# Seven pairs of transposes moved from TensorE to VectorE, and a head that runs zero matmuls and loads tile by tile, in a matmul with subtraction

## The chip, the cores and the metric

The kernel runs on one core of a Trainium2 chip. The metric is device microseconds of one execution, as the median of several runs. The profiled execution is one more run, and its span goes from its first to its last instruction.

## The reference

```python
def setup_inputs():
    batch, m, k, n = 16, 512, 1024, 768
    # x (16, 512, 1024), weight (1024, 768), sub_value (16, 512, 768), all float32
def reference(x, weight, sub_value):
    return (np.matmul(x, weight) - sub_value).astype(np.float32)
```

With batch and m flattened, this is an 8192 x 1024 by 1024 x 768 product, from which an 8192 x 768 array is subtracted. In bytes: 33.6 MB of x, 3.1 MB of weight and 25.2 MB of sub_value are read, and 25.2 MB of output are written.

## The kernel before

The 8192 rows are cut into 64 tiles of 128 rows ("m tiles", numbered by `mi`), and four neighbouring m tiles make a group (16 groups). TensorE contracts over partitions, so each tile of x has to be turned: ScalarE casts it from f32 to f16 (`cast`, L97), the engine that is to turn it sees pairs of f16 as one f32 word (so a tile is 128 x 512 words, four 128 x 128 blocks), TensorE transposes the four blocks against an identity matrix into PSUM (`transposes`, L105), and ScalarE copies the turned tile back to SBUF (L112). Even and odd k are then separate stripes of the turned tile. The weight is loaded so that it matches: each of its four chunks has even and odd rows side by side, and VectorE casts it to f16 (L76).

A tile's product is four chunks (`matmuls(mi, c)`), each of four matmuls of 128 x 384 (two stripes by two halves of n), summed in one of three PSUM buffers. `finish` (L144, VectorE) subtracts sub_value in place in its own SBUF tile `so_tile`, which is then stored.

The order on every engine is the order of the code (`keep` holds it). The head works on tiles 0, 1 and 2 together, chunk by chunk as the weights arrive. The main loop runs over `mi` from 3: at each first tile of a group SP issues the load of x three groups ahead (`XA`), of sub_value two groups ahead (`SA`), and a store `OA` groups behind; then come the four chunks of tile `mi`, with one transposed block of tile `mi + 2` (`TA`) behind each chunk; then the cast of tile `mi + 4` (`TA + CA`) and `finish(mi)`. All transfers are on SP's one queue. They take turns on eight completion semaphores, and the ninth is issued only when the first has landed. The x pool holds four groups, so a group's load also waits until ScalarE has cast the whole group four before it. `transposes_dve` exists but has no tile in `ON_DVE`.

Of the kernel before, what the change touches and what calls it, by code (L numbers as in the profile page):

```python
# [8 lines left out]
P = 128  # L9
Q = 32  # L10
F32 = mybir.dt.float32
F16 = mybir.dt.float16

S = 8
G = 4
XA, SA, OA = 3, 2, 1
TA = 2
CA = 2
HEAD = 3
ON_DVE = frozenset()  # L20


@with_exitstack
def kernel(
    ctx: ExitStack,
    tc: tile.TileContext,
    x: bass.AP,
    weight: bass.AP,
    sub_value: bass.AP,
    out: bass.AP,  # L30
):
    nc = tc.nc
    keep = tc.keep_in_program_order

    x_flat = x.flatten_outer_dims()
    sub_flat = sub_value.flatten_outer_dims()
    out_flat = out.flatten_outer_dims()

    M_TOT, K = x_flat.shape
    _, N = weight.shape  # L40
    n_mt = M_TOT // P
    n_g = n_mt // G
    NS = N // 2
    KW = K // 2
    n_c = KW // P

    x_s = x_flat.rearrange("(s p j) k -> s p j k", p=P, j=S)
    sub_s = sub_flat.rearrange("(s p j) n -> s p j n", p=P, j=S)
    out_s = out_flat.rearrange("(s p j) n -> s p j n", p=P, j=S)
    w_c = weight.rearrange("(c p r) n -> c p r n", p=P, r=2)  # L50

    def rows(view, mi, n):
        return view[mi // S][:, mi % S : mi % S + n]

    const_pool = ctx.enter_context(tc.tile_pool(name="const", bufs=1))
    w_pool = ctx.enter_context(tc.tile_pool(name="w_pool", bufs=1))
    x_pool = ctx.enter_context(tc.tile_pool(name="x_pool", bufs=4))
    x16_pool = ctx.enter_context(tc.tile_pool(name="x16_pool", bufs=CA + 2))
    xt_pool = ctx.enter_context(tc.tile_pool(name="xt_pool", bufs=TA + 3))
    so_pool = ctx.enter_context(tc.tile_pool(name="so_pool", bufs=6))  # L60
    psum_t_pool = ctx.enter_context(tc.tile_pool(name="psum_t", bufs=2, space=bass.MemoryType.PSUM))
    psum_o_pool = ctx.enter_context(tc.tile_pool(name="psum_o", bufs=3, space=bass.MemoryType.PSUM))

    ident = const_pool.tile([P, P], F32)
    make_identity(nc, ident)


    w_sb = w_pool.tile([P, n_c, 2, N], F16)

    x_t, so_t, x16_t, xt_t, ps_t, po_t = {}, {}, {}, {}, {}, {}  # L70

    def load_w(c):
        st = so_pool.tile([P, 2, N], F32, name="w_stage", tag="so_tile")
        keep(nc.sync.dma_start(out=st, in_=w_c[c]))
        for r in range(2):
            keep(nc.vector.tensor_copy(out=w_sb[:, c, r], in_=st[:, r]))  # L76

    def load_x(mi, n):
        g, j = divmod(mi, G)
        if j == 0:  # L80
            x_t[g] = x_pool.tile([P, G, K], F32, name="x_tile")
        keep(nc.sync.dma_start(out=x_t[g][:, j : j + n], in_=rows(x_s, mi, n)))

    def load_sub(mi, n):
        g, j = divmod(mi, G)
        if j == 0:
            so_t[g] = so_pool.tile([P, G, N], F32, name="so_tile")
        keep(nc.sync.dma_start(out=so_t[g][:, j : j + n], in_=rows(sub_s, mi, n)))

    def store(mi, n):  # L90
        g, j = divmod(mi, G)
        keep(nc.sync.dma_start(out=rows(out_s, mi, n), in_=so_t[g][:, j : j + n]))

    def cast(mi):
        g, j = divmod(mi, G)
        x16_t[mi] = x16_pool.tile([P, K], F16, name="x16_tile")
        keep(nc.scalar.copy(out=x16_t[mi], in_=x_t[g][:, j]))  # L97


    def transposes(mi):  # L100
        def one(c):
            def f():
                if c == 0:
                    ps_t[mi] = psum_t_pool.tile([P, K], F16, name="psum_t")
                keep(nc.tensor.transpose(  # L105
                    ps_t[mi].bitcast(F32)[:, c * P : (c + 1) * P],
                    x16_t[mi].bitcast(F32)[:, c * P : (c + 1) * P],
                    ident,
                ))
                if c == n_c - 1:  # L110
                    xt_t[mi] = xt_pool.tile([P, K], F16, name="xt_tile")
                    keep(nc.scalar.copy(out=xt_t[mi], in_=ps_t.pop(mi)))  # L112
                    x16_t.pop(mi)
            return f
        return [one(c) for c in range(n_c)]

    def transposes_dve(mi):
        xt_t[mi] = xt_pool.tile([P, K], F16, name="xt_tile")
        src = x16_t.pop(mi).bitcast(F32).rearrange("p (c q) -> p c q", c=n_c)
        dst = xt_t[mi].bitcast(F32).rearrange("p (c m) -> p c m", c=n_c)  # L120
        for a in range(P // Q):
            for b in range(P // Q):
                keep(nc.vector.transpose(
                    dst[b * Q : (b + 1) * Q, :, a * Q : (a + 1) * Q],
                    src[a * Q : (a + 1) * Q, :, b * Q : (b + 1) * Q],
                ))

    def matmuls(mi, c):
        if c == 0:
            po_t[mi] = psum_o_pool.tile([P, 2, 512], F32, name="psum_o")  # L130
        for r in range(2):
            for h in range(2):
                keep(nc.tensor.matmul(  # L133
                    po_t[mi][:, h, :NS],
                    xt_t[mi][:, 2 * P * c + r : 2 * P * (c + 1) : 2],
                    w_sb[:, c, r, h * NS : (h + 1) * NS],
                    start=(c == 0 and r == 0),
                    stop=(c == n_c - 1 and r == 1),
                ))

    def finish(mi):
        g, j = divmod(mi, G)
        o = so_t[g][:, j].rearrange("p (h n) -> p h n", h=2)
        keep(nc.vector.tensor_tensor(  # L144
            out=o, in0=po_t.pop(mi)[:, :, :NS], in1=o, op=mybir.AluOpType.subtract
        ))


    load_x(0, 1)
    for c in range(n_c):  # L150
        load_w(c)
        if c < 2:
            load_x(c + 1, 1)
    load_x(3, 1)
    load_sub(0, 2)
    load_x(4, 2)
    load_sub(2, 2)
    load_x(6, 2)
    for g in range(2, XA):
        load_x(g * G, G)  # L160
        if g - 1 < SA:
            load_sub((g - 1) * G, G)

    for mi in range(HEAD):
        cast(mi)
        for f in transposes(mi):
            f()
        for c in range(max(mi, 1)):
            matmuls(mi, c)
        if mi:  # L170
            for t in range(mi + 1):
                matmuls(t, mi)
    for c in range(HEAD, n_c):
        for mi in range(HEAD):
            matmuls(mi, c)
    for mi in range(HEAD):
        finish(mi)
    for mi in range(HEAD, HEAD + TA):
        cast(mi)
        for f in transposes(mi):  # L180
            f()
    for mi in range(HEAD + TA, HEAD + TA + CA):
        cast(mi)


    for mi in range(HEAD, n_mt):
        g, j = divmod(mi, G)
        if j == 0 or mi == HEAD:
            if g + XA < n_g:
                load_x((g + XA) * G, G)  # L190
            if g + SA < n_g:
                load_sub((g + SA) * G, G)
            if g >= OA:
                store((g - OA) * G, G)
        t = mi + TA
        tr = []
        if t < n_mt and t not in ON_DVE:
            tr = transposes(t)
        for c in range(n_c):
            matmuls(mi, c)  # L200
            if tr:
                tr[c]()
        if mi + TA + CA < n_mt:
            cast(mi + TA + CA)
        finish(mi)
        if t + 1 < n_mt and t + 1 in ON_DVE:
            transposes_dve(t + 1)
    for g in range(n_g - OA, n_g - 1):
        store(g * G, G)
    store(n_mt - G, G - 2)  # L210
    store(n_mt - 2, 1)
    store(n_mt - 1, 1)
# [30 lines left out]
```

## Time and profile before

| what | value |
|---|---|
| median of 3 runs | 220.35 us (220.28 to 220.97) |
| the profiled execution's own time | 221.13 us |
| its span | 219.4 us |
| mean granted TensorE clock | 0.982 |
| TensorE matmuls busy | 202.2 us (92%) |
| ScalarE busy | 126.7 us (58%) |
| VectorE busy | 65.2 us (30%) |
| packets of SP's queue, share of 16 DMA engines over the span | 94.4% |
| bytes moved | 87.22 MB, of them 61.87 read and 25.17 written |

Busy shares are means over the whole span. Matmuls overlap, so the 332 ns that a matmul takes is more than its share of TensorE's time, which is read from the distance between starts. A transfer "lands" when the last of its 16 parts has landed, one part for each DMA engine.

### The profile page before, as it was taken

The numbers are of one execution on the slowest core, as the hardware profiler recorded it, in microseconds if no ns is written. First come the engines' busy times: TensorE is split into PE (matmuls) and PEld (weight loads), VectorE is DVE, ScalarE is ACT, GpSimd is POOL, SyncE is SP. The second block draws the span as 40 slices with busy tenths as digits, with TensorE's granted clock in tenths as the row PEclk, the third lists the DMA queues.
The fourth block names the chain that finished last, engine by engine and source line by source line (L and its number), as shares of the span: only waits on it lengthen the run. The fifth ranks groups of instructions, "written<-read, shape, count | busy, mean of one in ns | idle before, by whom it ended". The sixth has DMA issues, their size and how long they took to land.

```text
span 219.4 us, 3000 instructions
## 1 busy us (share of the span) xinstructions
PE 202.2 (92%) x1280; PEld 138.3 (63%) x1280; DVE 65.2 (30%) x72; ACT 126.7 (58%) x129; POOL 0.7 (0%) x6
## 2 busy tenths in 40 slices
PE   0687589999999999999999999999999999999991
PEld 0344356677667766677667766677667766676660
DVE  0330403322333323333233332233322333223331
ACT  3523526666766667666667666676666766667510
POOL 1000000000000000000000000000000000000000
PEclk9999958999999999999999999999999999999999
DMA  6999999999999999999999999999999999995543
GB/s 226 422 416 420 438 427 416 432 426 418 423 419 429 423 430 427 426 425 435 427 428 430 426 417 428 435 426 424 425 434 407 429 433 426 424 424 211 251 179 143
DMA packets 8509, 87.22 MB, mean 398 GB/s; under 512 B 944, under 2 KB 944, under 8 KB 2608
## 3 DMA queue, kind: packets, MB, share of 16 engines
q1 hardware_dynamic: 8496, 87.04, 94.4%
q8 instruction: 10, 0.16, 0.3%
q14 instruction: 3, 0.02, 0.0%
HBM read 61.87 MB, written 25.17 MB: 397 GB/s over the span
## 4 chain that ended last, share of the span: by engine, by line
PE 92%; ACT 3%; DMA 2%; issue 1%; DVE 0%
PE psum_o L133 78%; PE psum_t L105 14%; DMA x_tile<-in_x_dram 2%; ACT x_tile L97 1%; ACT xt_tile L112 1%; DVE so_tile L144 0%
## 5 line engine op out<-in xcount | busy, mean ns | idle before, releaser
L133 PE MATMUL psum_o<-w_sb,xt_tile 128*128 128x384 f16 x1024 | 198.2, 332 | 3.3 <-ACT xt_tile L112 3.3
L133 PEld LDWEIGHTS <-xt_tile 128*128 128x128 f16 x1024 | 101.5, 99 | 50.0 <-ACT xt_tile L112 4.5
L112 ACT COPY xt_tile<-psum_t 128x1024 f16<-128x1024 f16 x64 | 64.8, 1012 | 80.7 <-PE psum_t L105 80.7
L144 DVE TENSOR_TENSOR so_tile<-psum_o,so_tile 128x768 f32<-128x768 f32 x64 | 61.1, 958 | 138.9 <-PE psum_o L133 138.9
L105 PE MATMUL psum_t<-ident,x_tile 128*128 128x128 f32 x256 | 69.4, 282 | 9.4 <-ACT x_tile L97 9.4
L97 ACT CAST x_tile<-x_tile 128x1024 f16<-128x1024 f32 x64 | 67.0, 1048 | 2.8 <-DMA x_tile<-in_x_dram 2.8
L105 PEld LDWEIGHTS psum_t<-ident,x_tile 128*128 128x128 f32 x256 | 37.0, 146 | 26.2 <-issue 6.8
L76 DVE CAST w_sb<-w_stage 128x768 f16<-128x768 f32 x8 | 4.1, 557 | 11.8 <-DMA w_stage<-in_weight_dram 11.8
L97 ACT ACT_TABLE_LOAD x1 | 1.3, 1283 | 0.7 <-PEq L227 0.7
masks.py:199 POOL TENSOR_SCALAR_AFFINE_SELECT ident<-ident 128x128 f32<-128x128 f32 x1 | 0.3, 294 | 0.1
masks.py:197 POOL MEMSET ident<- 128x128 f32 x1 | 0.2, 206 | 0.3 <-POOLq L227 0.3
L227 POOL MEMSET const-bfloat16-1.0<- 128x1 bf16 x1 | 0.1, 102 | 0.0
L227 POOL MEMSET const-uint8-127<- 128x1 uint8 x1 | 0.1, 102 | 0.0
L227 POOL MEMSET const-float32-0.0<- 128x1 f32 x1 | 0.1, 99 | 0.2 <-issue 0.2
L227 POOL MEMSET const-float32-1.0<- 128x1 f32 x1 | 0.1, 99 | 0.0
## 6 DMA issues: line engine op xcount, KB each, us to landing
x_tile<-in_x_dram SPq DMA_DIRECT2D x14, 2048.0 KB, 25.7
so_tile<-in_sub_value_dram SPq DMA_DIRECT2D x15, 1536.0 KB, 28.9
out_dram<-so_tile SPq DMA_DIRECT2D x15, 1536.0 KB, 21.9
w_stage<-in_weight_dram SPq DMA_DIRECT2D x4, 768.0 KB, 8.6
x_tile<-in_x_dram SPq DMA_DIRECT2D x4, 512.0 KB, 7.3
x_tile<-in_x_dram SPq DMA_DIRECT2D x2, 1024.0 KB, 14.4
so_tile<-in_sub_value_dram SPq DMA_DIRECT2D x2, 768.0 KB, 13.7
out_dram<-so_tile SPq DMA_DIRECT2D x1, 768.0 KB, 3.3
```

The lines of the kernel that those rows point to most:

```text
L76: keep(nc.vector.tensor_copy(out=w_sb[:, c, r], in_=st[:, r]))
L97: keep(nc.scalar.copy(out=x16_t[mi], in_=x_t[g][:, j]))
L105: keep(nc.tensor.transpose(ps_t[mi].bitcast(F32)[:, c * P : (c + 1) * P], x16_t[mi].bitcast(F32)[:, c * P : (c + 1) * P], ident,))
L112: keep(nc.scalar.copy(out=xt_t[mi], in_=ps_t.pop(mi)))
L133: keep(nc.tensor.matmul(po_t[mi][:, h, :NS], xt_t[mi][:, 2 * P * c + r : 2 * P * (c + 1) : 2], w_sb[:, c, r, h * NS : (h + 1) * NS], start ...
L144: keep(nc.vector.tensor_tensor(out=o, in0=po_t.pop(mi)[:, :, :NS], in1=o, op=mybir.AluOpType.subtract))
L227: nc = _bacc.Bacc("TRN2", target_bir_lowering=False, num_devices=1)
```

## The change

Four things change.

- **Pairs on VectorE.** Tiles 18 and 19, 24 and 25, and so on to 54 and 55 (`ON_DVE`, seven pairs) are cast into one tile `x16p_tile` and transposed by VectorE in 16 instructions, each turning a 32 x 32 block of words at the same place of all eight 128 x 128 blocks of the pair. They are cast seven tiles ahead (`LEAD_DVE`) where the others are cast four ahead. The instructions are put behind `finish`, four in each of four iterations (`PER`). The turned pair is written to SBUF directly, without PSUM and without ScalarE's copy.
- **Head.** TensorE runs 25 matmuls on zeros (`idle`, 13, 5, 4 and 3 of them) at places where the real work still waits, and the chunks of tiles 0 to 3 stand in another order: the cast and the transposes of tile 3 come ahead of the last chunk of tiles 0 to 2.
- **Loads.** The first eight transfers stay. Behind them x and sub_value come by one tile in turn, then by two (`HEAD_TRANSFERS`), where before they came by two and by four.
- **Stores.** `OA` goes from 1 to 2: a group's store stands one section later on SP's queue. The pool of `so_tile` gets a seventh buffer.

```diff
-XA, SA, OA = 3, 2, 1
+XA, SA, OA = 3, 2, 2
+LEAD_DVE = 7
+PER = 4
-ON_DVE = frozenset()
+ON_DVE = frozenset(range(18, 60, 6))
+HEAD_TRANSFERS = [('x', 0, 1), ('w', 0, 0), ('x', 1, 1), ('w', 1, 0), ('x', 2, 1), ('w', 2, 0), ('w', 3, 0), ('x', 3, 1), ('s', 0, 1), ('x', 4, 1), ('s', 1, 1), ...
...
     def cast(mi):
         g, j = divmod(mi, G)
+        first = mi - mi % 2
+        if first in ON_DVE:
+            if mi == first:
+                x16_t["pair", mi] = x16p_pool.tile([P, 2, K], F16, name="x16p_tile")
+            keep(nc.scalar.copy(out=x16_t["pair", first][:, mi - first], in_=x_t[g][:, j]))
+            return
...
     def transposes_dve(mi):
+        x16 = x16_t.pop(("pair", mi)).bitcast(F32).rearrange("p j (c q) -> p (j c) q", c=n_c)
+        xt_p = xtp_pool.tile([P, 2, K], F16, name="xtp_tile")
+        xt_t[mi], xt_t[mi + 1] = xt_p[:, 0], xt_p[:, 1]
+        xt = xt_p.bitcast(F32).rearrange("p j (c m) -> p (j c) m", c=n_c)
+        def one(a, b):
+            def f():
                 keep(nc.vector.transpose(
-                    dst[b * Q : (b + 1) * Q, :, a * Q : (a + 1) * Q],
-                    src[a * Q : (a + 1) * Q, :, b * Q : (b + 1) * Q],
+                    xt[b * Q : (b + 1) * Q, :, a * Q : (a + 1) * Q],
+                    x16[a * Q : (a + 1) * Q, :, b * Q : (b + 1) * Q],
                 ))
...
+    idle(13)
+    cast(0)
+    transpose_tile(0)
+    idle(5)
+    matmuls(0, 0)
...
+    cast(3)
+    transpose_tile(3)
     for mi in range(HEAD):
+        matmuls(mi, 3)
         finish(mi)
...
-        if t < n_mt and t not in ON_DVE:
-            tr = transposes(t)
+        tr = transposes(t) if t < n_mt and t - t % 2 not in ON_DVE else []
...
-        if mi + TA + CA < n_mt:
-            cast(mi + TA + CA)
+        for t in range(mi, n_mt):
+            if t - lead(t) == mi:
+                cast(t)
         finish(mi)
-        if t + 1 < n_mt and t + 1 in ON_DVE:
-            transposes_dve(t + 1)
+        if mi + LEAD_DVE - 1 in ON_DVE:
+            waiting += transposes_dve(mi + LEAD_DVE - 1)
+        for f in waiting[:PER]:
+            f()
+        del waiting[:PER]
```

The prediction speaks of SP's queue around the last load of x. Before, it stands there so (`so_tile_1043` is group 10, `x_tile_1493` group 15, `so_tile_1495` group 14):

```order
L92 DMA out_0_dram<-so_tile_1043 128x3072
L82 DMA x_tile_1493<-in_x_dram 128x4096
L88 DMA so_tile_1495<-in_sub_value_dram 128x3072
L92 DMA out_0_dram<-so_tile_1156 128x3072
L88 DMA so_tile_1606<-in_sub_value_dram 128x3072
```

After, the same place is this (`so_tile_991` is group 9, `x_tile_1548` group 15, `so_tile_1550` group 14):

```order
L97 DMA out_0_dram<-so_tile_991 128x3072
L87 DMA x_tile_1548<-in_x_dram 128x4096
L93 DMA so_tile_1550<-in_sub_value_dram 128x3072
L97 DMA out_0_dram<-so_tile_1102 128x3072
L93 DMA so_tile_1675<-in_sub_value_dram 128x3072
```

Eleven stores stood ahead of the last load of x, and now ten do.

On ScalarE casts and copies took turns. After, around the pair 48 and 49, it is so (`x_tile_1100` is group 11, `x_tile_1205` group 12, whose first two tiles are the pair; the copies are those of tiles 44, 45 and 46):

```order
L108 CAST x16_tile_1374<-x_tile_1100 128x1024
L105 CAST x16p_tile_1376<-x_tile_1205 128x1024
L123 COPY xt_tile_1401<-psum_t_1384 128x1024
L108 CAST x16_tile_1403<-x_tile_1100 128x1024
L105 CAST x16p_tile_1376<-x_tile_1205 128x1024
L123 COPY xt_tile_1434<-psum_t_1417 128x1024
L108 CAST x16_tile_1436<-x_tile_1100 128x1024
L123 COPY xt_tile_1470<-psum_t_1453 128x1024
```

The cast of tile 48 now stands ahead of the copy of tile 44, at iteration 41; before it stood at iteration 44.

On VectorE there were only `finish` instructions in the main loop. After, one pair is:

```order
L160 TENSOR_TENSOR so_tile_759<-psum_o_1036,so_tile_759 128x768
L137 STREAM_TRANSPOSE xtp_tile_1064<-x16p_tile_1033 32x8x32 x4
L160 TENSOR_TENSOR so_tile_759<-psum_o_1069,so_tile_759 128x768
L137 STREAM_TRANSPOSE xtp_tile_1064<-x16p_tile_1033 32x8x32 x4
L160 TENSOR_TENSOR so_tile_864<-psum_o_1105,so_tile_864 128x768
L137 STREAM_TRANSPOSE xtp_tile_1064<-x16p_tile_1033 32x8x32 x4
L160 TENSOR_TENSOR so_tile_864<-psum_o_1134,so_tile_864 128x768
L137 STREAM_TRANSPOSE xtp_tile_1064<-x16p_tile_1033 32x8x32 x4
```

Sixteen transposes are added for each pair, four behind each of four `finish` instructions; two `finish` instructions without transposes follow before the next pair.

More of the change, by code (lines that the diff above doesn't have):

```diff
@@ L15 @@
 G = 4
-XA, SA, OA = 3, 2, 1
+XA, SA, OA = 3, 2, 2
 TA = 2
 CA = 2
+LEAD_DVE = 7
+PER = 4
 HEAD = 3
-ON_DVE = frozenset()
+ON_DVE = frozenset(range(18, 60, 6))
+HEAD_TRANSFERS = [('x', 0, 1), ('w', 0, 0), ('x', 1, 1), ('w', 1, 0), ('x', 2, 1), ('w', 2, 0), ('w', 3, 0), ('x', 3, 1), ('s', 0, 1), ('x', 4, 1), ('s', 1, 1), ('x', 5, 1), ('s', 2, 1), ('x', 6, 1), ('s', 3, 1), ('x', 7, 1), ('x', 8, 2), ('s', 4, 2), ('x', 10, 2), ('s', 6, 2)]
 @with_exitstack
@@ L59 @@
     xt_pool = ctx.enter_context(tc.tile_pool(name="xt_pool", bufs=TA + 3))
-    so_pool = ctx.enter_context(tc.tile_pool(name="so_pool", bufs=6))
+    x16p_pool = ctx.enter_context(tc.tile_pool(name="x16p_pool", bufs=2))
+    xtp_pool = ctx.enter_context(tc.tile_pool(name="xtp_pool", bufs=2))
+    so_pool = ctx.enter_context(tc.tile_pool(name="so_pool", bufs=7))
     psum_t_pool = ctx.enter_context(tc.tile_pool(name="psum_t", bufs=2, space=bass.MemoryType.PSUM))
@@ L117, in transposes_dve @@
     def transposes_dve(mi):
[L118 to L122, printed above, removed]
+        x16 = x16_t.pop(("pair", mi)).bitcast(F32).rearrange("p j (c q) -> p (j c) q", c=n_c)
[4 more added lines that the diff above has]
+            def f():
                 keep(nc.vector.transpose(
-                    dst[b * Q : (b + 1) * Q, :, a * Q : (a + 1) * Q],
-                    src[a * Q : (a + 1) * Q, :, b * Q : (b + 1) * Q],
-                ))
+                    xt[b * Q : (b + 1) * Q, :, a * Q : (a + 1) * Q],
+                    x16[a * Q : (a + 1) * Q, :, b * Q : (b + 1) * Q],
+                ))
+            return f
+        return [one(a, b) for a in range(P // Q) for b in range(P // Q)]
     def matmuls(mi, c):
@@ L195 @@
         t = mi + TA
-        tr = []
-        if t < n_mt and t not in ON_DVE:
-            tr = transposes(t)
+        tr = transposes(t) if t < n_mt and t - t % 2 not in ON_DVE else []
         for c in range(n_c):
```

61 lines of the change are left out of this document (32 added, 29 removed).

## The prediction, blind

> **What bounds the kernel now.** I read the page first: busy shares, the slices, the queues, the chain that ended last.
>
> ```profile
> span 219.4 us, 3000 instructions
> ...
> PE 202.2 (92%) x1280; PEld 138.3 (63%) x1280; DVE 65.2 (30%) x72; ACT 126.7 (58%) x129; POOL 0.7 (0%) x6
> ...
> DMA  6999999999999999999999999999999999995543
> GB/s 226 422 416 420 438 427 416 432 426 418 423 419 429 423 430 427 426 425 435 427 428 430 426 417 428 435 426 424 425 434 407 429 433 426 424 424 211 251 179 143
> ...
> q1 hardware_dynamic: 8496, 87.04, 94.4%
> ...
> PE 92%; ACT 3%; DMA 2%; issue 1%; DVE 0%
> ```
>
> TensorE sets the end. But the DMA row says that a second resource is nearly as full: the queue is at 9 from the second slice to the 36th, and only the last four slices have room. The sums by stage say it more sharply.
>
> ```profile
> core 0: us, PE busy (x) PEld busy (x) DVE busy (x) ACT busy (x) POOL busy (x), PEclk, DMA share, GB/s
> 50.00:200.00 150.00, 150.00 (x990) 105.13 (x989) 46.94 (x49) 96.72 (x99) 0.00 (x0) 1.00 1.01 425
> 200.00:219.40 19.40, 14.95 (x97) 9.75 (x94) 5.75 (x6) 5.94 (x6) 0.00 (x0) 0.97 0.42 172
> ...
> 28.00:34.00 6.00, 5.88 (x20) 3.33 (x21) 0.96 (x1) 1.90 (x3) 0.00 (x0) 0.50 1.01 426
> ```
>
> From 50 to 200 us both TensorE (150 of 150) and the DMA engines (share 1.01, 425 GB/s) are full. A group of four tiles moves 2.10 MB of x, 1.57 of sub_value and 1.57 of output, 5.24 MB, which at 425 GB/s is 12.3 us. What TensorE needs for it is in the chain, whose parts are start, length and work:
>
> ```profile
> 23.43 0.89 issue
> 24.32 1.06 ACT x_tile L97
> ...
> 33.08 1.19 PE psum_o L133 x4
> 34.27 0.11 PE psum_t L105
> 34.38 0.65 PE psum_o L133 x4
> ...
> 209.75 5.21 PE psum_o L133 x32
> ...
> 214.98 0.96 DVE so_tile L144
> ```
>
> A chunk is 0.65 us and a transposed block 0.11, so a tile is 2.6 us without transposes and 3.04 with them, and a group 12.2 us. TensorE and the queue run level. TensorE is last only because it starts late: tile 4 begins at 33.08 us. From there 60 x 2.6 + 58 x 0.44 gives 214.6, and the chain shows 214.98.
>
> **The floor of the queue.** Where single transfers stand, by issue and time to landing (tile 3 of x, then the load of group 12, of group 15, and the last store):
>
> ```profile
> L82 SPq DMA_DIRECT2D x_tile<-in_x_dram x1: 452/452/452, 4.5 to 4.5; - x1
> ...
> DMA to landing us min/median/max: 11.6/11.6/11.6
> ...
> L82 SPq DMA_DIRECT2D x_tile<-in_x_dram x1: 327/327/327, 120.7 to 120.7; - x1
> ...
> DMA to landing us min/median/max: 25.8/25.8/25.8
> ...
> L82 SPq DMA_DIRECT2D x_tile<-in_x_dram x1: 327/327/327, 157.1 to 157.1; - x1
> ...
> DMA to landing us min/median/max: 26.4/26.4/26.4
> ...
> L92 SPq DMA_DIRECT2D out_dram<-so_tile x1: 332/332/332, 216.0 to 216.0; - x1
> ...
> DMA to landing us min/median/max: 2.3/2.3/2.3
> ```
>
> So x of tile 3 lands at 16.1 us, x of group 12 at 146.5, x of group 15 at 183.5, and the last store at 218.3, 1.1 before the end of the span. The first eight transfers are 5.24 MB and end with tile 3; the change leaves them, so 81.8 MB of the 87.04 remain after 16.1 us. Two rates can be had. The mean of moved bytes, 425 GB/s, gives 192.5 us, a last landing at 208.6. The landings themselves give less: between tile 3 and group 15 the queue's order puts 60 tiles of x, 56 of sub_value and 44 of stores, 70.8 MB in 167.4 us or 423 GB/s, since a transfer lands with its slowest part; that gives 193.4 us and 209.5. I take 209.5, because the end also waits for the slowest part. If the queue never idles after the change, the kernel can't end earlier than this, whatever TensorE gains.
>
> **The change part by part.**
>
> Head and loads. The price of a slow head is in the rows above: TensorE waits for ScalarE around 23 to 28 us, and then its granted clock is 0.50 for six us, since the cast of tile 4 (24.32) stands behind the copy of tile 3, which waits for all chunks of tiles 0 to 2. After, tile 3 is turned ahead of those. From x of tile 3 at 16.1, ScalarE and TensorE alternate: cast 1.05, four blocks 0.5, copy 1.0, and the same for tile 4 (x lands about 18.3, after 0.92 MB more), then the cast of tile 5: 16.1 + 1.05 + 0.5 + 1.0 + 1.05 + 0.5 + 1.0 + 1.05 = 22.3. The chunks of tile 3 stand behind that with three distances of 0.76, and tile 4 begins at about 24.9, 8.2 us earlier than before. The zero matmuls fill waits of TensorE; at the slow clock the 13 could delay tile 0 by about a microsecond, which the wait for x at 16.1 hides. Smaller loads keep eight transfers of some 0.45 MB in flight, 8 us of work, so I cost them at nothing.
>
> Pairs, TensorE and ScalarE.
>
> ```profile
> L105 PE MATMUL psum_t<-ident,x_tile 128*128 128x128 f32 x256 | 69.4, 282 | 9.4 <-ACT x_tile L97 9.4
> L97 ACT CAST x_tile<-x_tile 128x1024 f16<-128x1024 f32 x64 | 67.0, 1048 | 2.8 <-DMA x_tile<-in_x_dram 2.8
> L112 ACT COPY xt_tile<-psum_t 128x1024 f16<-128x1024 f16 x64 | 64.8, 1012 | 80.7 <-PE psum_t L105 80.7
> ```
>
> TensorE loses 14 x 4 blocks at 0.11, 6.2 us of its path. ScalarE loses 14 copies, 14.2 us, but it has 80.7 us of idle time ahead of them, so this is worth nothing. TensorE alone would end at 24.9 + 60 x 2.6 + 44 x 0.44 = 200.3, 14.7 us earlier.
>
> Pairs, VectorE. 112 transposes of 256 words are added; no row has one. Rows to bound it by:
>
> ```profile
> 6.65 1.03 DVE L76 CAST w_sb<-w_stage 128x768 f16<-128x768 f32 x2 [6.65 <-DMA w_stage<-in_weight_dram]
> ...
> 21.67 2.69 DVE L144 TENSOR_TENSOR so_tile<-psum_o,so_tile 128x768 f32<-128x768 f32 x3 [5.78 <-PE psum_o L133]
> ...
> L144 DVE TENSOR_TENSOR so_tile<-psum_o,so_tile 128x768 f32<-128x768 f32 x64 | 61.1, 958 | 138.9 <-PE psum_o L133 138.9
> ```
>
> Back to back, a subtraction of 768 columns costs (2.69 - 0.96) / 2 = 0.87 us and a cast of 768 some 0.5. A third of the cast's columns gives 0.17, the lower end; 0.87, if fewer columns bring nothing, is the upper. I take 0.33: a third of the subtraction's 0.87 is 0.29, and a little for starting. Four of them and a subtraction are 2.3 us in an iteration of 2.6 to 3.04, so VectorE keeps up. The deadline: they start about 3.2 us after tile 12 ends (copy and two casts on ScalarE, where the second of the pair is cast), three more subtractions stand between them, and tile 18 is due 14.3 us after tile 12: 3.2 + 16d + 2.9 = 14.3 at d = 0.51. Below that the pairs cost nothing.
>
> The Trainium skill speaks against this part. VectorE: DVE Perf Modes, The three transpose paths and Rules for kernel authors, says that VectorE transposes only within 32 x 32 blocks (311 ns for 128 columns against TensorE's 390), and to give a 128 x 128 transpose to TensorE. Doubled for 256 columns this is at most 0.62 us as an estimate; each pair would then be 1.8 us late, and TensorE would end near 212.6, a time of 217.9. By my 0.33 nothing is late. No run here shows the instruction yet.
>
> Earlier casts. This is where a stall goes.
>
> ```profile
> ACT x_tile L97 <- DMA x_tile<-in_x_dram: 2.8, 1, 2.8
> ```
>
> Before, ScalarE waited once for x, at the start. After, a pair is cast seven tiles ahead, three tiles (9 us) earlier. The worst is tile 48, first of group 12, cast at iteration 41. By its own work TensorE ends tile 41 at 24.9 + 38 x 2.6 + 28 x 0.44 = 136.0. Group 12 lands at 146.5 less one store (1.57 MB, 3.7 us, since `OA` moves one behind it), 142.8. ScalarE stands 6.8 us, and the copy of tile 44 is queued behind: 142.8 + 1.05 + 1.0 = 144.9, when TensorE was done with tiles 42 and 43 at 142.1. TensorE waits 2.8 us there in all (some 0.9 of it falls already at tile 36, the same way). It ends at 203.1.
>
> Stores. `OA` puts stores behind loads: x earlier by 3.7 us, stores later. At the end groups 11 to 15 are still to be stored when sub_value has landed, and all of them are finished when their turn comes: tile 59 ends near 192.7, and its group's turn begins two groups (7.4 us) before 209.5, at about 202. The last tile is subtracted at 204.1, its turn is near 208. So the queue does not idle. The seventh buffer costs nothing: the load that reuses it stands eight transfers behind the store that frees it, and SP waits for that one anyway.
>
> **The sum.** TensorE's path: last landing 203.1 + 3.3 (from 214.98 to 218.3 before) = 206.4. The queue's path: 209.5. The later decides, 209.5 + 1.1 = 210.6 of span. The profiled execution took 221.13 for 219.4, 1.7 more: 212.3. It lies 0.8 above the median of 220.35, so I forecast **211.5**. Of TensorE's 14.7 us the queue swallows about two fifths.
>
> **The rivals.**
>
> *The queue moves faster, TensorE decides.* For it: slices of 438 and 435 GB/s. Against: the mean of 150 us is 425 at share 1.01. Then 206.4 + 1.1 + 1.7 - 0.8 = 208.4. Beside it, the Trainium skill, DMA: Bandwidth & Descriptors, Where 436 GB/s comes from, gives a ceiling of 435 GB/s into SBUF; at that an estimate is 188.0 us for the 81.8 MB, a last landing at 204.1, and TensorE's path decides. The trace's 425 is 2% below it. The same section names about 358 for transfers between HBM and SBUF, which the trace contradicts.
>
> *TensorE loses more than 2.8 us.* Waits for x could take its clock, as at 28 to 34 us, where six us at 0.50 lose three. One such loss ends at 206.1, a landing at 209.4, hidden by the queue; two give 212.4, a time of 214.4. For it: ScalarE's long wait. Against: each wait here is under 3 us. 213 to 216.
>
> *VectorE becomes the bound: slower.* At d over 0.51 each pair adds 16 (d - 0.51) to TensorE's path, which absorbs the waits for x. TensorE then ends at 200.3 + 7 x 16 (d - 0.51). It would pass the old 215 at d = 0.64 and reach 240 at the upper end 0.87, a time of about 246 (3.3 + 1.1 + 1.7 - 0.8 = 5.3 more); at 0.70 it is 221.6, a time of 226.9. For it: strided writes across partitions, seen in no row. Against: a third of the columns.
>
> *The zero matmuls do not open the clock.* Then the slow distances (a chunk was 1.19 to 1.28 at clock 0.50) make tile 4 start at about 27.5. That is 2.6 us later, less than the 2.8 that TensorE waits for group 12 anyway, and the end does not move: 211.5 again. Even a start at 30 ends TensorE at 205.4, a landing at 208.7, below 209.5. So the head's clock is not a case of its own.
>
> **How the numbers follow.** The queue sets the end: 0.72 (210.6 by the landing at 208.6, and up to 213 if it idles now and then). TensorE sets it early: 0.06 (208.4). TensorE late by waits: 0.14 (213 to 216). VectorE: 0.08, of which slower than before 0.05. The range reaches from 208.4 to 214.5, which holds the first two and half of the third, 0.85. A difference of 0.3% (0.7 us) is about what can be told from no change. Faster 0.93, same 0.02, slower 0.05.
>
> **What would show it.** Right: DMA at 9 up to the last slice or two, ending in a transfer; 50 copies on ScalarE and waits of casts for x of several us near tiles 36 and 48; tile 4 at about 25 us and no 0.5 clock near 30; transposes near 0.33 us; TensorE idle for about 3 us in the main loop. Wrong: slices of the queue below 9 in the middle, transposes over 0.5 us, or TensorE waiting for turned pairs.

## The result and the profile after

The changed kernel takes 212.76 us (median of 4 runs, 212.62 to 213.83) against 220.31 before: a ratio of 0.966 (95% interval 0.9625 to 0.9698), 7.6 us faster. In a later set of six runs it took 212.60 us, ratio 0.965 (0.961 to 0.968). The forecast was 211.5, with a range from 208.4 to 214.5.

The same parts of the page as before:

```profile
span 211.1 us, 3028 instructions
...
PE 198.0 (94%) x1249; PEld 129.7 (61%) x1249; DVE 114.0 (54%) x186; ACT 112.7 (53%) x115; POOL 0.7 (0%) x6
...
PEclk9999999999999999999999999999999999999995
DMA  6999999999999999999999999999999999999994
GB/s 217 422 413 406 415 418 446 418 425 440 414 429 420 433 426 423 435 421 435 424 422 432 424 434 422 435 420 432 425 429 435 414 428 416 434 412 433 428 409 162
...
q1 hardware_dynamic: 9360, 87.04, 98.2%
```

The DMA row is at 9 through the 39th slice, where before it ended with the 36th. The same bytes move at the same rate, and of four last slices with room in the queue (22 us) one is left. TensorE's clock does not drop before the end. By stage, in the columns shown before:

```profile
50.00:200.00 150.00, 147.47 (x950) 98.29 (x948) 96.67 (x163) 82.99 (x86) 0.00 (x0) 1.00 1.01 427
200.00:211.10 11.10, 3.97 (x25) 2.16 (x23) 1.91 (x2) 0.00 (x0) 0.00 (x0) 0.78 0.71 293
```

TensorE now idles in the middle (147.47 of 150) and the queue does not. The chain (start, length, work) at the start of tile 4 and at the end, and the last store by issue and time to landing:

```profile
24.98 0.11 PE psum_t L116
25.09 0.65 PE psum_o L149 x4
...
198.77 5.21 PE psum_o L149 x32
...
204.00 0.96 DVE so_tile L160
```

```profile
L97 SPq DMA_DIRECT2D out_dram<-so_tile x1: 333/333/333, 205.0 to 205.0; - x1
...
DMA to landing us min/median/max: 5.2/5.2/5.2
```

Tile 4 begins at 25.09 us instead of 33.08, TensorE ends at 203.98 instead of 214.96, and yet the span ends only 8.3 us earlier: the last store, issued at 205.0, lands after 5.2 us, where before it took 2.3. It stands in the queue behind what is still to be moved.

The waits, as who waited for whom, total, times and longest:

```profile
ACT x16p_tile L105 <- DMA x_tile<-in_x_dram: 20.5, 5, 7.3
ACT x_tile L108 <- DMA x_tile<-in_x_dram: 7.3, 6, 2.6
PE psum_o L149 <- ACT xt_tile L123: 1.7, 2, 1.0
PE psum_o L149 <- DVE xtp_tile L137: 0.6, 2, 0.3
```

The pairs' casts, which are seven tiles ahead, now wait for x in the main loop, where before no cast did. (Of the 7.3 us of the other casts, 7.0 fall before 25 us.) The longest waits are 7.3 us at tile 48, 6.9 at tile 36 and 4.9 at tile 24. Little of it reaches TensorE: it stands idle for 2.5 us between 50 and 200 us.

### The profile page after: what moved, and what is told of

Same layout as the page of the kernel before. It is cut to its first block, busy times and chain, and to the rows that moved or that the text cites. A ratio compares the mean times of both kernels' runs of the same rounds, so it can differ in the third digit from the quotient of the medians.

```text
span 211.1 us, 3028 instructions
## 1 busy us (share of the span) xinstructions
PE 198.0 (94%) x1249; PEld 129.7 (61%) x1249; DVE 114.0 (54%) x186; ACT 112.7 (53%) x115; POOL 0.7 (0%) x6
## 2 busy tenths in 40 slices
DMA packets 9374, 87.23 MB, mean 413 GB/s; under 512 B 1040, under 2 KB 1040, under 8 KB 3728
## 4 chain that ended last, share of the span: by engine, by line
DMA 49%; PE 33%; ACT 9%; DVE 3%; SPq 2%; issue 1%; ACTq 0%
DMA x_tile<-in_x_dram 49%; PE psum_o L149 28%; PE psum_t L116 5%; ACT x_tile L108 4%; ACT xt_tile L123 3%; ACT x16p_tile L105 2%; DVE xtp_tile L137 2%; DVE so_tile L160 1%; SPq L79 1%; SPq L87 1%; ACTq L105 0%
## 5 line engine op out<-in xcount | busy, mean ns | idle before, releaser
L149 PE MATMUL psum_o<-w_sb,xt_tile 128*128 128x384 f16 x800 | 145.9, 326 | 1.7 <-ACT xt_tile L123 1.7
L149 PEld LDWEIGHTS <-xt_tile 128*128 128x128 f16 x800 | 78.1, 98 | 42.0 <-ACT xt_tile L123 2.8
L123 ACT COPY xt_tile<-psum_t 128x1024 f16<-128x1024 f16 x50 | 50.6, 1012 | 58.7 <-PE psum_t L116 58.0
L137 DVE STREAM_TRANSPOSE xtp_tile<-x16p_tile 32x256 f32<-32x256 f32 x112 | 48.8, 436 | 22.4 <-ACT x16p_tile L105 20.6
L108 ACT CAST x_tile<-x_tile 128x1024 f16<-128x1024 f32 x50 | 51.7, 1049 | 7.3 <-DMA x_tile<-in_x_dram 7.3
L116 PE MATMUL psum_t<-ident,x_tile 128*128 128x128 f32 x200 | 52.4, 274 | 2.3 <-ACT x_tile L108 1.9
L149 PE MATMUL psum_o<-w_sb,xtp_tile 128*128 128x384 f16 x224 | 42.9, 326 | 0.6 <-DVE xtp_tile L137 0.6
L116 PEld LDWEIGHTS psum_t<-ident,x_tile 128*128 128x128 f32 x200 | 27.5, 141 | 16.5 <-ACT x_tile L108 4.7
L149 PEld LDWEIGHTS <-xtp_tile 128*128 128x128 f16 x224 | 21.7, 98 | 10.9 <-DVE xtp_tile L137 1.4
L105 ACT CAST x16p_tile<-x_tile 128x1024 f16<-128x1024 f32 x14 | 14.6, 1046 | 20.5 <-DMA x_tile<-in_x_dram 20.5
```

Of the source, the lines that this page charges most:

```text
L105: keep(nc.scalar.copy(out=x16_t["pair", first][:, mi - first], in_=x_t[g][:, j]))
L116: keep(nc.tensor.transpose(ps_t[mi].bitcast(F32)[:, c * P : (c + 1) * P], x16_t[mi].bitcast(F32)[:, c * P : (c + 1) * P], ident,))
L137: keep(nc.vector.transpose(xt[b * Q : (b + 1) * Q, :, a * Q : (a + 1) * Q], x16[a * Q : (a + 1) * Q, :, b * Q : (b + 1) * Q],))
L149: keep(nc.tensor.matmul(po_t[mi][:, h, :NS], xt_t[mi][:, 2 * P * c + r : 2 * P * (c + 1) : 2], w_sb[:, c, r, h * NS : (h + 1) * NS], start ...
```

## Experiments

My theory is that the queue of transfers ends the kernel: whatever takes TensorE's path below the queue's is worth nothing more. The rivals are that the gains of the parts add up, that the place of the stores made the gain, that VectorE or TensorE still bounds it, and that the queue is slow only because the engines work beside it. The kernel before was timed beside each set at 220.02 us (first four), 220.08 (next four) and 220.45 (the last).

### Without the zero matmuls

```diff
     def idle(n):
-        for _ in range(n):
+        for _ in range(0):
```

> The changed kernel without its 25 matmuls on zeros. Queue theory (the transfers end the kernel, last landing 210.2 us): tile 4 starts at 25 to 27.5 instead of 25.1, TensorE waits that much less for group 12 of x, the time stays 212.8 within 0.5. Rival (the zero matmuls hold the clock and each microsecond of the head reaches the end): a slow clock before about 17 us or again near 25, the end 2 to 5 us later, 215 to 218.

Measured: 212.79 us, ratio 0.9676 (0.9652 to 0.9701). The timeline of TensorE shows the first chunk without the zeros, and in the changed kernel:

```profile
8.02 1.46 PE L149 MATMUL psum_o<-w_sb,xt_tile 128*128 128x384 f16 x4 [1.10 <-ACT xt_tile L123]
```

```profile
7.52 0.82 PE L149 MATMUL psum_o<-w_sb,xt_tile 128*128 128x384 f16 x4
```

The chain without the zeros shows tile 4:

```profile
25.02 0.11 PE psum_t L116
25.13 0.65 PE psum_o L149 x4
```

The first chunk takes 1.46 us where the changed kernel's takes 0.82, so the zeros do bring the full clock earlier. But tile 4 begins at 25.13 against 25.09: the chain runs through x of tile 3, which lands at 16 us in both, and this hides the slow beginning. The zero matmuls are worth nothing here, neither at the end nor at tile 4, and my allowance of up to 27.5 for tile 4 was too wide.

### Without the pairs

```diff
-ON_DVE = frozenset(range(18, 60, 6))
+ON_DVE = frozenset()
```

> The changed kernel with no tile on VectorE: all 64 tiles turned by TensorE, new head, loads and stores kept. Queue theory: TensorE's own path ends at 25.1 + 60 x 2.6 + 58 x 0.44 = 206.6, a last landing at 209.9, the queue's path 210.2, so 212.8 within 0.7; the waits of ScalarE for x in the main loop are gone. Rival (the gains of head and pairs add up, and TensorE decides): the 6.2 us of the pairs come back, 219.

Measured: 212.90 us, ratio 0.9677 (0.9652 to 0.9702). The chain's end:

```profile
201.44 5.21 PE psum_o L149 x32
...
206.68 0.96 DVE so_tile L160
```

TensorE ends 2.7 us later than with the pairs, at 206.65, where the sum had 206.6, and the time does not change. Beside the new head the pairs on VectorE are worth nothing. The rival's 219 is ruled out. The two paths now end level: the last store, issued at 207.7, lands after 2.6 us, where it took 5.2 with the pairs and 2.3 before the change, so the queue holds little else by then. Without the pairs TensorE's path has no room left against the queue's; with them it has some 3 us.

### Only the pairs

The kernel before, with `ON_DVE`, `LEAD_DVE` and `PER` of the changed one.

```diff
-ON_DVE = frozenset()
+ON_DVE = frozenset(range(18, 60, 6))
```

> The kernel before with only the seven pairs on VectorE: old head, old loads, old place of the stores, six buffers for sub_value. Queue theory: tile 4 at 33.1, TensorE ends at 33.1 + 60 x 2.6 + 44 x 0.44 + 0.5 = 208.9, last landing 212.2, so TensorE decides by 2 us: 214.8 within 0.8, a gain of 5.5 of the 7.6. With the run without pairs the gains of the two halves then add to about 13, not to 7.6. Rival (the gains add up to 7.6): if the run without pairs shows 6 of it, this one shows about 1.5, 218.8.

Measured: 214.79 us, ratio 0.9766 (0.9724 to 0.9809), with 214.8 forecast. That it agrees so closely is in part luck: the four runs go from 213.85 to 215.90, and in the profiled one, the fastest, tile 4 begins at 32.01 instead of 33.1 and TensorE ends 1.3 us before the 208.9 of the sum. Alone, then, the pairs gain 5.2 us, and the rest of the change without them gains 7.1. Together that would be 12.3, and the whole change gains 7.6. In the chain TensorE ends at 207.64:

```profile
202.43 5.21 PE psum_o L149 x32
...
207.67 0.96 DVE so_tile L160
```

### The queue alone

All casts, transposes, matmuls and subtractions are left out; the transfers keep their order, and sub_value is stored unchanged.

```diff
+    for g in range(n_g):
+        if g == 0 or g + XA < n_g:
             if g + XA < n_g:
                 load_x((g + XA) * G, G)
+        if g + SA < n_g:
+            load_sub((g + SA) * G, G)
+        if g >= OA:
+            store((g - OA) * G, G)
```

> Only the transfers of the changed kernel, in its order of the queue: x, weight and sub_value are loaded and the unchanged sub_value is stored; the casts, the transposes, the product and the subtraction are left out. Queue theory: the queue alone takes what the whole kernel takes, last landing 209 to 210.2, 211.5 to 212.8. Rival (the queue is slowed by the engines' traffic, or waits for them): 205 or less.

Measured: 211.53 us, ratio 0.9613 (0.9584 to 0.9642). The page, and the sums by stage (span, no TensorE, clock, share and rate of the queue):

```profile
span 210.6 us, 118 instructions
...
DMA  6999999999999999999999999999999999999993
...
50.00:200.00 150.00, 0.00 (x0) 1.00 1.01 427
```

The bare transfers take 99.4% of the time of the changed kernel, at the same 427 GB/s, and the rival's 205 is ruled out. The 1.2 us between them is more than the noise (no bare run took over 212.40, no run of the changed kernel under 212.50), so the engines cost the queue up to 0.6%; by what, no run shows. The profiled execution, with 210.6 the span that the prediction had worked out from two landings, is the slowest of the four. The spans of the others are 209.6 to 209.9, nearer to the 209.7 that the rate of moved bytes would have given (208.6 + 1.1). The floor is shown to about 1 us, and not which of the two rates is the better.

### Less to move

```diff
-            if g >= OA:
+            if g >= OA + 2:
```

The stores of the first two groups are left out.

> The changed kernel without the stores of the first two groups (3.15 MB, 7.4 us of the queue; these rows of the output are left unwritten). Queue theory: x of the later groups lands 7.4 us sooner, so ScalarE's and TensorE's waits for it go, TensorE ends at its own 200.5, last landing 203.8 against the queue's 202.8: 206.4 within 1. Rival (VectorE or TensorE bound the kernel, the full queue is only a companion): 212.8 as before.

Measured: 206.45 us, ratio 0.9383 (0.9356 to 0.9410). With 3.15 MB less to move the kernel is 6.3 us faster, and TensorE and VectorE do the same work as before.

```profile
50.00:200.00 150.00, 150.00 (x972) 101.13 (x971) 98.21 (x164) 83.64 (x86) 0.00 (x0) 1.00 1.00 422
```

TensorE is full again in the middle: its idle time in the changed kernel was the queue's doing. The rival's 212.8 is ruled out. The chain's end:

```profile
195.86 4.73 PE psum_o L149 x29
200.59 0.02 issue
200.61 0.96 DVE so_tile L160
```

TensorE ends at 200.59 (forecast 200.5), and the last store lands 2.3 us after its issue, as in the kernel before: now TensorE's path ends the kernel. From the beginning of tile 4, at 25.36 here, TensorE needs 175.2 us, and in the changed kernel 178.9: the waits for x cost it about 3.7 us there.

### Stores ahead of the loads

```diff
-XA, SA, OA = 3, 2, 2
+XA, SA, OA = 3, 2, 1
```

> The changed kernel with OA = 1, so that a group's store stands ahead of the next loads again; same bytes. Queue theory: the queue's path stays at 210.2, but x of group 12 lands 3.7 us later, TensorE waits that much more and ends at 207.7, last landing 211.0: 213.6 within 0.6, so the place of the stores is worth at most 1 us. Rival (the place of the stores is what made the kernel faster): 216 or more.

Measured: 213.85 us, ratio 0.9721 (0.9687 to 0.9754). The wait of the cast of tile 48 on ScalarE, here and in the changed kernel:

```profile
146.48 1.05 ACT L105 CAST x16p_tile<-x_tile 128x1024 f16<-128x1024 f32 x1 [7.18 <-DMA x_tile<-in_x_dram]
```

```profile
142.85 1.05 ACT L105 CAST x16p_tile<-x_tile 128x1024 f16<-128x1024 f32 x1 [7.30 <-DMA x_tile<-in_x_dram]
```

One store is 3.6 us of landing (forecast 3.7). The chain's end:

```profile
202.40 5.21 PE psum_o L149 x32
207.61 0.02 issue
```

TensorE ends at 207.61 (forecast 207.7), and the last store lands 2.3 us after its issue, so that here TensorE's path ends the kernel. It is about 1 us slower than the changed kernel; the intervals overlap, so that this microsecond is no more than likely. A place of the stores worth 3 us or more is ruled out.

### Twice the transposes

```diff
-        return [one(a, b) for a in range(P // Q) for b in range(P // Q)]
+        return [one(a, b) for a in range(P // Q) for b in range(P // Q) for _ in range(2)]
-PER = 4
+PER = 8
```

> The changed kernel with each VectorE transpose issued twice (32 for a pair, eight behind each finish). By the deadline of a pair (start 3.2 us after a tile ends, three subtractions between, 14.3 us to the tile that needs it) 16 x 0.89 + 6.1 - 14.3 = 6.0 us late in each of seven pairs: TensorE ends at 243, 249 within 5. Rival by busy shares (VectorE at 54%, twice the transposes is 77% of the span, below full): no change, 212.8.

Measured: 268.54 us, ratio 1.2197 (1.2156 to 1.2239). The busy share is 61%, and VectorE is the bound nevertheless. The waits of TensorE, then two stages (TensorE's clock is the third number from the end):

```profile
PE psum_o L149 <- DVE xtp_tile L137: 39.4, 7, 5.6
PE psum_o L149 <- DVE so_tile L160: 4.5, 7, 0.6
...
72.00:79.00 7.00, 5.75 (x20) 3.18 (x21) 2.97 (x5) 0.00 (x0) 0.00 (x0) 0.51 1.01 430
79.00:99.00 20.00, 14.76 (x94) 9.54 (x92) 16.87 (x34) 9.72 (x10) 0.00 (x0) 1.00 1.00 426
```

Seven waits of 5.6 us each (forecast 6.0) confirm the deadline. But the time missed the forecast by 20 us, and TensorE ends at 262.74 where the sum had 243. The sum lacked what follows a wait. After each of the seven the clock is half for 3.4 or 6.8 us, as from 72 to 79. These stretches are 41.0 us together, TensorE was busy for 33.0 of them, and at half clock it lost about half of that, 16.5 us. Another 4.5 us are waits for product buffers, which VectorE's subtractions free (the second row). With the waits for turned pairs 2.6 us shorter than forecast, this gives 18.4 of the 19.7 us.

### Only the order of the head

The kernel before, with the cast and the transposes of tile 3 ahead of the last chunk of tiles 0 to 2.

```diff
+    cast(3)
+    transpose_tile(3)
     for mi in range(HEAD):
+        matmuls(mi, 3)
         finish(mi)
```

> The kernel before with only the order of the head's work changed on TensorE and ScalarE (tile 3 cast and turned ahead of the last chunk of tiles 0 to 2): no zero matmuls, no pairs, old loads, OA = 1, six buffers. Queue theory: x of tiles 4 and 5 comes as one load, landing about 20.5, so tile 4 starts near 27, TensorE ends at 27 + 181.5 = 208.5, last landing 211.8: 214.4 within 1. Rival (the new loads, the zero matmuls or OA = 2 are needed for the head's gain): 217 or more.

Measured: 215.89 us (214.30 to 217.31), ratio 0.9809 (0.9751 to 0.9867), 1.5 above the forecast.

```profile
20.47 1.05 ACT x_tile L97
...
24.75 1.28 PE psum_o L133 x4
26.03 0.21 PE psum_t L105
26.24 1.28 PE psum_o L133 x4
27.52 0.13 PE psum_t L105
27.64 0.65 PE psum_o L133 x4
...
28.41 0.65 PE psum_o L133 x4
```

The order alone gains 4.2 us, and the median lies between the forecast and the rival's 217. Tiles 4 and 5 come as one load, so the cast of tile 4 starts at 20.47 (18.67 in the changed kernel), TensorE waits longer, and two chunks run at half clock, 1.28 instead of 0.65. Tile 4 begins at 28.41, where the sum had 27. From the chunk at 24.75 to tile 4 are 3.66 us, and at full clock it would be three distances of 0.76, 2.28 us: the drop costs 1.4 us, and it is what my sum lacked. The other runs agree: the one with a mean clock of 1.000 took 214.30, and the one with 0.982 took 217.31. In the profiled run TensorE ends at 209.7, where the sum had 208.5. Without zero matmuls but with the new loads the clock held (first experiment), so the loads are the likely difference; the new loads and `OA` were not tried apart from each other.

### A store cut in two

```diff
-    store(n_mt - G, G - 2)
+    for p0, p1 in ((0, 120), (120, 128)):
+        g, j = divmod(n_mt - G, G)
+        keep(nc.sync.dma_start(out=rows(out_s, n_mt - G, 2)[p0:p1], in_=so_t[g][p0:p1, j : j + 2]))
```

> The changed kernel with the store of tiles 60 and 61 cut by partitions into 120 and 8, to see whether the queue's path can be shortened where its parts end unevenly (in the changed kernel the 16 parts of the last store land between 207.1 and 210.2 us). If one and the same part is the late one, and the cut takes this store's 1.8 us off it, the last landing is about 1 us sooner, 211.8. If the late parts change from transfer to transfer, or the cut does not take the late one out, 212.8 or a little more. The Trainium skill, DMA: Bandwidth & Descriptors, Why a DMA increments its semaphore by 16 and not by 1, says that a transfer over 120 partitions would go on 15 of the 16 engines.

> The changed kernel itself, for comparison on the same chip: 212.8 within 0.4.

Measured: 213.07 us, ratio 0.9675 (0.9642 to 0.9708), beside the changed kernel's 212.60. The cut gained nothing. The count of packets in the changed kernel, and with the cut:

```profile
DMA packets 9374, 87.23 MB, mean 413 GB/s; under 512 B 1040, under 2 KB 1040, under 8 KB 3728
```

```profile
DMA packets 9381, 87.23 MB, mean 413 GB/s; under 512 B 1047, under 2 KB 1047, under 8 KB 3735
```

The 65 transfers of the changed kernel have 1040 packets under 512 B, 16 for each. With the cut there are 1047 for 66 transfers, so the two new stores have 23 between them, which fits 15 parts for the first, as expected, and 8 for the second. Whether the late parts change or the cut missed them stays open; no run here shows on which engines the parts went.

## Why the prediction was right, and where its sizes were off

- **The queue's path decides.** Forecast: last landing 209.5, span 210.6. Measured: 210.2 and 211.1. The last store's 5.2 us from issue to landing and the two runs with a changed queue (bare, and with less to move) show that this path decides. Of the two rates the slower one, from landings, was nearer here, but the bare queue's spans of 209.6 to 210.6 do not decide between them.
- **TensorE's path.** Tile 4 was forecast for 24.9 and began at 25.09. x of group 12 was forecast for 142.8, and the cast that waited for it began at 142.85, after 7.3 us of waiting (forecast 6.8). TensorE's end was forecast for 203.1 and was 203.98: tile 4 was 0.2 us late, and the waits for x cost about 3.7 instead of 2.8. The prediction placed them at tiles 36 and 48; the cast of tile 24 waited too, for 4.9 us.
- **Hidden gains.** TensorE's path became 11.0 us shorter and the span 8.3. The runs without zeros and without pairs stay within 0.2 us of the changed kernel, as a queue that ends last, or level with TensorE's path, demands. So the seven pairs add nothing to what the rest of the change had gained.
- **VectorE's transposes were mis-sized.** I took 0.33 us, a third of a subtraction and a little. The group of the changed kernel has 0.44:

```profile
L137 DVE STREAM_TRANSPOSE xtp_tile<-x16p_tile 32x256 f32<-32x256 f32 x112 | 48.8, 436 | 22.4 <-ACT x16p_tile L105 20.6
```

  and four in a row take 1.78 us, so they do not overlap as subtractions do. It stayed below the deadline of 0.51 with 0.07 to spare, where the forecast had 0.18, and TensorE waited 0.6 us in all for turned pairs. That the pairs were in time was closer than the forecast had it. The Trainium skill's figure (VectorE: DVE Perf Modes, The three transpose paths) doubled, 0.62, was above the measured value; the measurement decides.
- **Why 212.8 and not 211.5.** The span was 0.5 us longer. The other 0.8 is in the step from span to median: I took the profiled execution of before to lie 0.8 above the median and carried that over. After, the profiled execution took 212.88 us, 0.1 above its median.
- **The rivals.** A faster queue did not come: 427 GB/s over the same stage. The clock did not drop in the main loop. The zero matmuls did open the clock, and without them the end did not move, as that rival's sum had it. VectorE did not bind, but doubling its transposes turned it into the bound, on the side of the 0.51 that the deadline had set.

## What to carry to other kernels

Where a transfer queue and an engine are both near full, work out the queue's own end from the bytes left and two landings; no shortening of the engine's path gets below it, and gains of several edits do not add. Test such a floor by running the transfers alone. For work moved to an engine with idle time, compare its length from the first input to the moment that the result is needed, not its busy share: at 61% busy VectorE cost 56 us.

## What the runs showed of the hardware

- VectorE transposed 32 partitions by 256 f32 words in 0.436 us, 0.445 apart back to back, while 768-column subtractions overlapped by about 0.09 us.
- Matmuls on zeros brought TensorE to its full clock as others do: the chunk at 7.52 us after them ran in 0.82 us, and without them the chunk at 8.02 took 1.46. The Trainium skill, TensorE: Matmul & The Clock Gate, Part 1: The HAM clock gate, says that activity releases the clock; this agrees.
- After waits of TensorE of about 1 us in the main loop the clock stayed full; those of 5.6 us in the run with doubled transposes were followed by half clock for 3.4 or 6.8 us.
- The transfers ran at 427 GB/s from 50 to 200 us with the engines at work and without them.
- The last store took 5.2 us from issue to landing behind a full queue, and 2.3 in the kernel before, whose queue had room at the end.
- The 16 parts of one transfer landed within 0.7 us of each other at the start of the changed kernel, and within 3.0 us for its last store.
